# Gates by seven half products and queries channel-major in a hybrid DeltaNet, retention and gated-MLP block

## The chip, the cores and the metric

The kernel runs on one core of a Trainium2 chip. The metric is the device time of one execution in microseconds (us), as the median of several timed runs. One further execution is recorded by the profiler.

The engines are named as in the profile: PE multiplies matrices (PEld is its weight load), DVE and ACT and POOL do the elementwise work, and SP issues most of the DMA transfers. ACT issues the others on a queue of its own.

## The reference

One decoder block over 2048 tokens of width 1024, all in float32:

```python
n = rms_norm(x, attn_norm_w)
gq, gk, gv, gg, ga, gb, rq, rk, rv, rg = split(n @ w_in)      # 512 columns each; ga, gb: 4
o_gdn = gated_deltanet(gq, gk, gv, gg, ga, gb)   # 4 heads of 128
o_ret = retention(rq, rk, rv, rg)                # 4 heads of 128
h = x + concat(o_gdn, o_ret) @ w_out
n2 = rms_norm(h, mlp_norm_w)
g, u = split(causal_conv3(n2 @ w_up))            # 2816 columns each
h = h + (silu(g) * u) @ w_down
return rms_norm(h, final_norm_w)
```

- `gated_deltanet` runs a causal convolution of four taps and silu over q, k and v, normalizes each head's q and k to length 1, and applies the gated delta rule in chunks. Inside a chunk a unit triangular matrix is inverted; from chunk to chunk a 128x128 state per head is carried along. Its output is `rms(o) * norm_w * silu(gg)`.
- `retention` rotates q and k by position (pairs of neighbouring channels, cosine and sine tables) and applies a linear recurrence with a fixed decay per head. Its output is `rms(o) * silu(rg)`.
- `gg` and `rg` together are the 1024 columns of gates that this case is about.

## The kernel before

**Precision.** PE's fast format keeps fewer bits than float32, so every large operand is split into a high and a low part, and a product takes three passes (`mm3`, L116 to L118, and the same three in `tokmajor`, L399 to L401): high times high, high times low, low times high. A split is a copy by ACT and a subtraction by DVE.

**Blocks and items.** The tokens are worked in four blocks of 512 (`TB`), each of four tiles of 128. `mixers` makes, for each block, a dictionary of named items (functions that emit instructions). The string `ORDER` names them in the sequence in which they are emitted: `1p0` is item `p0` of block 1. `hybrid_block` walks this string. An item that needs weights has them loaded (`load_chunk`, into a pool of five `wc` tiles) when the weight-needing item ahead of it starts. A scheduler then places the instructions on each engine by priorities and modelled times, and sizes some pools, so the order on an engine follows `ORDER` only roughly. Matmuls of one block's projections, of the block before and of its output projection are interleaved with the recurrence.

The items of a block, in the order of the data:

- `pro` loads the transposed input (`xk`), scales it by the norm's weights and splits it into eight `n1` tiles (L387). It also sums squares of the input's rows and gets the inverse norm `r` of each token. `rrow`, the same numbers along a row on all partitions, is made by PE: four small matmuls of `r` with the identity (`rrp`, L373) and a copy by ACT.
- `k0`, `q0`, `kq`, `v0`: the retention's projections, token-major (`tokmajor`: tokens on partitions, up to 512 columns in a PSUM bank). Keys and queries are rotated by `rotate`: two DVE multiplications a head and tile (L769, L771) and an addition on POOL (L774).
- `dec`, `d0` to `d3`: decays; each head's decay matrix `D` comes by a broadcast from DRAM on ACT's queue (`D<-gdr`).
- `a0` to `a3` (`proj_kq`): the gated heads' keys and queries, channel-major (`chmajor`: channels on partitions, 512 tokens in a bank). DVE multiplies the bank by `rrow` (L520, `scaled`); the convolution and silu follow.
- `c0` to `c3` (`gdn_kq`): PE transposes keys and queries (`kqtr`, L555), and ACT sums the squares of each (L558); then the products of keys with keys and queries follow (L585). `f`, `e`: values.
- `b0`, `b1` (`gdn_base`): the triangle's inversion for two heads. POOL does its steps (L637, L639); the data goes through DRAM.
- `l0`, `l1` (`gdn_lvls`): the levels of the inverse above 32x32, with small matmuls on PE.
- `r00` to `r13` (`gdn_rec`): the recurrence, eight steps a block, each for two heads. A step is a chain: PE (`ks`), DVE (`kv`, L717), PE (`wps`, L724), DVE (`pers`, L727), PE (`sps`, L732), DVE (state, L734).
- `h0` to `h3`, `y0` to `y3` (`ret_head`, `ret_out`): retention. `ret_head` transposes keys and queries on PE (`rtr`, L826) and copies both by ACT (L827).
- `p0`, `p1` (`gates`): the gates, token-major, 512 columns each. ACT applies silu (L412).
- `g`, `G` (`gated`): norm times gate on DVE (`mix`, L435), transposed by PE (`mxt`, L437). Sums of token halves for the next item are made here (`co`).
- `W1` to `W7`: the output projection by seven products of half size in place of eight (a Strassen scheme over halves of tokens, of inner columns and of output columns). `load_v` makes the differences of weights when a product is first used: subtractions on POOL (`wvt`, L186), a split by ACT and DVE (L213, L214), and a copy kept in DRAM, from which the later blocks load.
- `N`: second norm, transposed, stored to DRAM for the MLP.

A projection's weight is loaded raw and split the first time (`wraw`, 512 KB loads). Its split form is kept in DRAM and loaded back for the later blocks (`wc<-wd`, 512 KB, high and low part). The gates' inner loop shows how often a tile is used: with 512 columns a `wc` tile holds one `k`, and serves 12 matmuls.

```python
for k in range(KT):
    wh, wl = wrow(w, k, ncol)
    for t in range(NT):
        ah, al_ = n1[k][:, 0, t * P:(t + 1) * P], n1[k][:, 1, t * P:(t + 1) * P]
        ps = pss[t][:, :ncol]
        PE.matmul(ps, ah, wh, start=(k == 0), stop=False)
        PE.matmul(ps, ah, wl, start=False, stop=False)
        PE.matmul(ps, al_, wh, start=False, stop=(k == KT - 1))
```

The mixers' items are followed by `mlp_up` (seven half products as well, about 1160 to 1940 us) and `mlp_down` (to the end). The products `W` of block 3 stand at the border.

Of the kernel before, what the change touches and what calls it, by code (L numbers as in the profile page):

```python
# [15 lines left out]
NW = 5  # L16
# [3 lines left out]
NVR = 4  # L20
NVV = 23
NWUR = 2
NST = 4
NUC = 6
NACC = 9
NWU = 9
NWV = 5
# [4 lines left out]
NPR = 2  # L32
NRAW = 3
NLATE = 3
NXR = 7
FD = 5
BUFS = {"n1": 8, "ykq": 5, "kv": 4, "NT": 6, "AT": 8, "o": 4, "n2s": 11, "xk": 2, "og": 1, "co": 7, "Cw": 7,
        "wx": 1, "wsq": 2, "wvr": 3, "wvt": 8, "ca": 8, "mix": 10, "D": 8, "rk": 6, "rq": 3, "rv": 8,
        "Ar": 1, "Nb": 7, "rot": 1, "rrow": 7}

ORDER = ("0pro 0k0 0v0 0dec 0d0 0a0 0c0 0f0 0e0 0q0 0d1 0a1 0c1 0f1 0a2 0e1 0d2 0c2 0f2 0h0 0y0 0b0 0h1 "
# [42 lines left out]
def hybrid_block(ctx, tc, x, xT, w_kq, w_v, w_g, w_rk, w_r0, w_r, w_o, w_u, w_d, cols, rows, fnr, masks, rot, out):  # L84
# [10 lines left out]
    nc.scalar.dma_start(colt, cols)  # L95
# [6 lines left out]
    gnw = colt[:, 204:205]  # L102
    mhalf = base[:, NCOL:NCOL + 16]
# [9 lines left out]
    def mm3(ps, pairs, first=True, chk=False):  # L113
        n = len(pairs)
        for i, (ah, al, bh, bl) in enumerate(pairs):
# [11 lines left out]
           for q in range(2) for i in range(1, 8)}  # L127

    items = mixers(ctx, tc, base, o, marks, drp, mm3, gamma, mhalf, n1w, n2w, gcw, gv127, epsr, gnw, n2d, hd,
                   x, xT, w_kq, w_v, w_g, w_rk, w_r0, w_r, w_o, rows, masks, rot)  # L130
# [28 lines left out]
def load_v(tc, pool, w, i, k, tags, kept=None, drp=None, held=None):  # L159
# [6 lines left out]
    if kept is not None and (i, k) in kept:  # L166
        v = mk("v", F32R)
        nc.sync.dma_start(v.bitcast(F32), kept[i, k])
        return v
# [35 lines left out]
    v = split_v(nc, mk("v", F32R), src)  # L205
    if kept is not None:
        kept[i, k] = drp.tile([P, 2, TB], F32, name=f"wo{i}_{k}", tag=f"wo{i}_{k}", bufs=1)
        nc.sync.dma_start(kept[i, k], v.bitcast(F32))
    return v
# [9 lines left out]
def mixers(ctx, tc, base, base_used, marks, drp, mm3, gamma, mhalf, n1w, n2w, gcw, gv127, epsr, gnw, n2d, hd,  # L219
           x, xT, w_kq, w_v, w_g, w_rk, w_r0, w_r, w_o, rows, masks, rot):  # L220
# [26 lines left out]
    mk = pc(4, P)  # L247
    nc.scalar.dma_start(mk, masks)
    ident = mk[:, 0, :]
    U = mk[:, 1, :]  # L250
    eye8 = mk[:, 2:].rearrange("p a b -> p (a b)").rearrange("p (c i) -> p c i", c=8)


    below = pc(P)
# [1080 lines left out]
```

## Time and profile before

| | before |
|---|---|
| median of 3 timed runs | 2457.25 us |
| the runs | 2455.92, 2462.43, 2457.25 us |
| span of the profiled execution | 2458.5 us |
| PE busy | 2397.2 us, 98% of the span |
| DVE, ACT, POOL busy | 65%, 41%, 22% |
| bytes moved by DMA | 607.29 MB, 247 GB/s on average |

How to read the profile's lines: `x` in front of a number counts instructions. In a line of a group, `out<-in` are names of tiles; behind them stand partitions x elements, the count, the total busy time and the mean duration of one in ns, then the idle time of the engine just ahead of them and what ended it. In a line of waits, `PE tok L399 <- ACT n L387: 9.6, 1, 9.6` says that the instructions of PE that write `tok` at line 399 waited for ACT's `n` of line 387: 9.6 us in total, over 1 wait, of which the longest took 9.6. In a line of a window, each engine's busy time stands beside its number of instructions; behind the engines come PEclk (the granted clock of PE, 1.00 is full), the share in which the DMA engines were busy, and GB/s. In a line of DMA issues, KB of each and median us from issue to landing stand last.

### The profile page before, as it was taken

What the parts mean: (1) busy time and instruction counts of PE and PEld (TensorE: products, weight loads), DVE (VectorE), ACT (ScalarE), POOL (GpSimd) and SP (SyncE); (2) the same over time, 40 slices, a digit from 0 to 9 for tenths busy, and PEclk for the clock granted to TensorE, in tenths of its full rate; (3) what the DMA queues carried; (4) which work ended last, traced back from release to release, by engine and by line L of the source; (5) the groups of instructions that cost most, each with busy time, mean ns of one, the idle gap of its engine ahead of it and who ended that gap; (6) DMA issues with size and microseconds to landing.
All of it is one profiled execution on the core that took longest, in us unless ns stands there. A gap on an engine that the chain in (4) does not pass through costs nothing.

```text
span 2458.5 us, 35801 instructions
## 1 busy us (share of the span) xinstructions
PE 2397.2 (98%) x12476; PEld 2016.0 (82%) x12476; DVE 1596.7 (65%) x3157; ACT 998.8 (41%) x2152; POOL 532.7 (22%) x877
## 2 busy tenths in 40 slices
PE   8998899999999999998999999999999999999998
PEld 7887788788888878887888888888888888888887
DVE  5855777444754563447888988896556577454674
ACT  6644535344442552336454344442122234332341
POOL 1354245621047105240000000000000002421030
PEclk9999999999999999999999999999999999999999
DMA  8856589674765656654998878877667778775773
GB/s 327 277 187 218 214 310 343 223 247 175 268 228 180 211 186 222 224 184 181 349 365 313 303 290 300 290 280 250 233 239 258 270 259 281 243 224 156 220 242 112
DMA packets 287477, 607.29 MB, mean 247 GB/s; under 512 B 41088, under 2 KB 121152, under 8 KB 287296
## 3 DMA queue, kind: packets, MB, share of 16 engines
q1 hardware_dynamic: 270720, 590.70, 68.7%
q10 hardware_dynamic: 16576, 14.30, 1.9%
q8 instruction: 98, 1.61, 0.3%
q14 instruction: 83, 0.68, 0.1%
HBM read 405.32 MB, written 199.59 MB: 246 GB/s over the span
## 4 chain that ended last, share of the span: by engine, by line
PE 84%; POOL 5%; DMA 4%; DVE 3%; issue 2%; ACT 2%; SPq 0%; ACTq 0%; POOLq 0%; DVEq 0%
PE p L116 11%; PE p L118 11%; PE p L117 11%; PE d L118 6%; PE d L116 6%; PE d L117 6%; PE tok L399 4%; PE tok L401 4%; PE tok L400 4%; PE chm L116 3%; PE chm L117 3%; PE chm L118 3%; POOL pers L639 2%; POOL pers L637 2%; PE wo L116 2%; PE wo L117 2%
## 5 line engine op out<-in xcount | busy, mean ns | idle before, releaser
L117 PE MATMUL p<-x,wu 128*128 128x512 f32 x1176 | 457.7, 389 | 0.0
L116 PE MATMUL p<-x,wu 128*128 128x512 f32 x1176 | 452.7, 389 | 0.0
L118 PE MATMUL p<-x,wu 128*128 128x512 f32 x1176 | 450.0, 389 | 0.0
L399 PE MATMUL tok<-wc,n 128*128 128x512 f32 (+2 forms) x768 | 276.5, 365 | 19.5 <-ACT n L387 9.6
L400 PE MATMUL tok<-wc,n 128*128 128x512 f32 (+2 forms) x768 | 276.6, 361 | 1.1 <-DVE wc L296 1.1
L401 PE MATMUL tok<-wc,n 128*128 128x512 f32 (+2 forms) x768 | 275.1, 361 | 0.0
L116 PEld LDWEIGHTS p<-x,wu 128*128 128x128 f32 x1176 | 220.8, 188 | 46.4 <-DVE uc L1053 0.4
L118 PEld LDWEIGHTS p<-x,wu 128*128 128x128 f32 x1176 | 220.8, 188 | 45.8
L117 PEld LDWEIGHTS p<-x,wu 128*128 128x128 f32 x1176 | 220.8, 188 | 45.8
L1095 DVE SCALAR_TENSOR_TENSOR acc<-uc,base,acc 128x1023 f32<-128x1023 f32 (+1 forms) x176 | 221.0, 1280 | 39.2 <-ACT acc L1092 38.9
L1053 DVE TENSOR_TENSOR uc<-p,uc 128x512 f32<-128x512 f32 x224 | 153.6, 689 | 134.8 <-PE p L118 131.6
L186 POOL TENSOR_TENSOR vt<-vr 128x512 f32<-128x512 f32 x44 | 66.0, 1504 | 633.0 <-DMA vr<-in_w_d 465.8
L399 PEld LDWEIGHTS tok<-wc,n 128*128 128x128 f32 x768 | 146.1, 191 | 41.0 <-ACT n L387 9.6
L117 PE MATMUL d<-v,uu 128*128 128x512 f32 x448 | 174.3, 389 | 0.0
L118 PE MATMUL d<-v,uu 128*128 128x512 f32 x448 | 174.3, 389 | 0.0
L116 PE MATMUL d<-v,uu 128*128 128x512 f32 x448 | 174.3, 389 | 0.0
L400 PEld LDWEIGHTS tok<-wc,n 128*128 128x128 f32 x768 | 146.5, 191 | 20.8 <-DVE wc L296 1.5
L401 PEld LDWEIGHTS tok<-wc,n 128*128 128x128 f32 x768 | 145.3, 191 | 19.8
L116 PE MATMUL chm<-n,wc 128*128 128x512 f32 x384 | 151.7, 395 | 0.0
L118 PE MATMUL chm<-n,wc 128*128 128x512 f32 x384 | 151.2, 394 | 0.0
L117 PE MATMUL chm<-n,wc 128*128 128x512 f32 x384 | 150.8, 393 | 0.0
L1092 ACT ACTIVATE acc<-uc,base 128x1024 f32<-128x1024 f32 x88 | 97.2, 1144 | 86.2 <-DVE uc L1053 45.1
(250 smaller groups left out, 4723.3 us busy)
## 6 DMA issues: line engine op xcount, KB each, us to landing
wu<-wu SPq DMA_DIRECT2D x308, 512.0 KB, 5.9
wc<-wd SPq DMA_DIRECT2D x168, 512.0 KB, 5.2
wv<-wo SPq DMA_DIRECT2D x84, 512.0 KB, 5.2
wd<-wc SPq DMA_DIRECT2D x60, 512.0 KB, 4.8
ur<-au SPq DMA_DIRECT2D x56, 512.0 KB, 5.5
wur<-in_w_u SPq DMA_DIRECT2D x44, 512.0 KB, 6.5
au<-st SPq DMA_DIRECT2D x88, 256.0 KB, 4.7
vr<-in_w_d SPq DMA_DIRECT2D x77, 256.0 KB, 5.0
```

What stands on the lines that cost most here:

```text
L116: PE.matmul(ps, ah, bh, start=(first and i == 0), stop=False, skip_group_check=chk)
L117: PE.matmul(ps, ah, bl, start=False, stop=False, skip_group_check=chk)
L118: PE.matmul(ps, al, bh, start=False, stop=(i == n - 1), skip_group_check=chk)
L186: POOL.tensor_tensor(tt[:, j], a, b_, op=ALU.subtract)
L399: PE.matmul(ps, ah, wh, start=(k == 0), stop=False)
L400: PE.matmul(ps, ah, wl, start=False, stop=False)
L401: PE.matmul(ps, al_, wh, start=False, stop=(k == KT - 1))
L637: POOL.tensor_tensor(tm[:, :, :n], Nb[:, j:j + 1, j + 1:].to_broadcast([P, 8, n]), X[:, :, j:j + 1].to_broadcast([P, 8, n]), op=ALU.mult)
L639: POOL.tensor_tensor(X[:, :, j + 1:], X[:, :, j + 1:], tm[:, :, :n], op=ALU.add)
L1053: add = lambda o, ps, a: DVE.tensor_tensor(o, ps, a, op=ALU.add)
L1092: ACT.activation(acc, u, AF.Copy, scale=mcw[:, ci, 2:3])
L1095: DVE.scalar_tensor_tensor(acc[:, t:], u[:, :T2 - t], w, acc[:, t:], op0=ALU.mult, op1=ALU.add)
```

## The change

**Gates.** In blocks 1 to 3 the items `P1`, `P4`, `P6`, `P7`, `P5` replace `p0` and `p1`. They compute all 1024 gate columns by the seven-product scheme (`seven`, `half_product`): a product covers 256 tokens, half of the inner columns and 512 gate columns, 24 matmuls. Its partial sums are put together by DVE from PSUM (`gate_ready` then applies silu). Three of the products read `n1` tiles; four read sums of token and channel halves, which items `S` and `T` (`combos`) make from a second load of the block's `xk`: ACT scales it, DVE adds, ACT and DVE split (tiles `sm`, `sc`). A 512 KB weight tile `wc<-kP` serves six matmuls. Block 0 keeps `p0` and `p1`, with weights read from the new layout.

**Weight differences.** `make` is a new stage: items `O0` to `O3` make all seven forms of the output weights, and `Q0` to `Q3` those of the gates, in block 0's and block 1's time: raw loads, four subtractions on POOL, seven splits by ACT and DVE and seven 512 KB stores to DRAM a stage (56 stores; `load_v` made 28, and 16 splits of the gates' weights were stored). `W1` to `W7` load from there in every block; `load_v` no longer keeps its results.

**Retention queries.** Items `q0`, `q1` compute them channel-major (`ret_q`): no transposes in `ret_head`. The rotation is three DVE operations and an addition on DVE for each head, with transposed tables `rotT`, scaled once a block by `rrow`. For that, each head's channels are permuted, even ones first. `k1` (256 columns) replaces `kq`. Values lie in tiles by token tile.

**Gated queries' norms.** `gdn_kq` no longer transposes the queries. ACT squares them channel-major, DVE transposes 32x32 squares and sums, and a small matmul in `gdn_lvls` (`fold`, `qss`) adds the four bands.

**Smaller edits.** `rrow` comes by a write of `r` to DRAM and a broadcast back on ACT's queue. The masks are loaded behind the fourth `n1` tile (`constants`). The first weights and the first input are loaded in halves, alternating (`first_x`). Pools are resized, and `ORDER` is new.

The diff, cut:

```diff
-NVR = 4
-NVV = 23
+NVR = 2
+NVV = 25
...
-        "wx": 1, "wsq": 2, "wvr": 3, "wvt": 8, "ca": 8, "mix": 10, "D": 8, "rk": 6, "rq": 3, "rv": 8,
-        "Ar": 1, "Nb": 7, "rot": 1, "rrow": 7}
+        "wx": 1, "wsq": 2, "wvr": 2, "wvt": 7, "ca": 9, "mix": 4, "D": 5, "rk": 8, "rq": 2, "rv": 10, "sm": 2,
+        "sc": 11, "wg": 2, "kt": 4, "Ar": 3, "Nb": 6, "rot": 1, "rrow": 4, "rT": 2}
...
+    def make(n, w, kk):
+        def f(_):
+            r = [unit(ap_, "wvr", [P, 2, TB], bufs=BUFS["wvr"]) for j in range(2)]
+            t = [unit(ap_, "wvt", [P, 2, TB], bufs=BUFS["wvt"]) for j in range(2)]
+            for j in range(2):
+                nc.sync.dma_start(r[j].rearrange("p a n -> p (a n)"), w[kk, :, 2 * j * TB:2 * (j + 1) * TB])
...
+            t1 = sub(0, b12, b11)
+            t2 = sub(1, b22, t1)
+            t4 = sub(2, b21, t2)
+            t3 = sub(3, b22, b12)
+            for i, src in ((1, b11), (2, b21), (4, t4), (6, t2), (7, t3), (5, t1), (3, b22)):
+                v = al("wg", [P, 2, TB], F32R)
+                ACT.activation(v[:, 0], src, AF.Copy)
+                DVE.tensor_tensor(v[:, 1], src, v[:, 0].bitcast(F32), op=ALU.subtract)
...
+                nc.sync.dma_start(d, v.bitcast(F32))
...
     def load_chunk(key, src):
+        if key[0] in "PV":
+            for kk in range(4):
+                wc = unit(wp, "wc", [P, 2, TB], F32R, bufs=NW)
+                marks["c"] = nc.sync.dma_start(wc.bitcast(F32), made[key[0]][key[1], kk])
...
-            ps = mbank("rrp")
-            for t in range(NT):
-                PE.matmul(ps[:, t * P:(t + 1) * P], r[:, t:t + 1].to_broadcast([P, P]), ident, start=True, stop=True)
+            rd = drp.tile([NT, P], F32, tag="rd", name="rd")
+            nc.scalar.dma_start(rd.rearrange("t p -> p t"), r)
             rrow = st["rrow"] = half(st, "rr", "rrow", 0)
-            ACT.activation(rrow, ps, AF.Copy)
+            nc.scalar.dma_start(rrow, rd.rearrange("t p -> (t p)").partition_broadcast(P))
...
+        def half_product(i, w, m, ps):
+            prs = []
+            for kk in range(4):
+                if i in (1, 2, 4):
+                    t0 = (2 * (i == 4) + m) * P
+                    n1 = st["n1"][2 * kk + (i != 1)]
+                    ah, al_ = n1[:, 0, t0:t0 + P], n1[:, 1, t0:t0 + P]
+                else:
+                    ah, al_ = (t[:, m * P:(m + 1) * P] for t in st["sc", i][kk])
+                prs.append((ah, al_, w[kk][:, 0], w[kk][:, 1]))
+            mm3(ps, prs, first=i not in (2, 3), chk=i in (2, 3))
...
+                        if i == 1:
+                            ACT.activation(c12[:, m], ps, AF.Copy)
+                        elif i == 2:
+                            ready(0, m, ps)
+                        elif i == 4:
+                            ACT.activation(c21[:, m], ps, AF.Copy)
+                        elif i == 6:
+                            DVE.tensor_tensor(c12[:, m], ps, c12[:, m], op=ALU.add)
+                        elif i == 7:
+                            DVE.tensor_tensor(c22[:, m], ps, c12[:, m], op=ALU.add)
+                            DVE.tensor_tensor(c21[:, m], c21[:, m], c22[:, m], op=ALU.add)
+                            ready(0, 2 + m, c21[:, m])
...
         def gdn_kq(h):
-                for i in range(2):
-                    ps = mbank("kqtr")
+                ps = mbank("kqtr")
...
+                q2 = al("ca", [P, 2, TB])
+                ACT.activation(q2[:, 0], ykq[:, 1], AF.Square)
+                DVE.transpose(q2[:, 1], q2[:, 0])
+                DVE.tensor_reduce(st["qr", h // 2][:, h % 2 * 16:(h % 2 + 1) * 16],
+                                  q2[:, 1].rearrange("p (a d) -> p a d", d=32), axis=mybir.AxisListType.X, op=ALU.add)
...
         def gdn_lvls(hs):
+                ps = mbank("qss")
+                PE.matmul(ps[:, :32], fold, st["qr", hs[0] // 2], start=True, stop=True)
...
-        def ret_kq1(w):
...
+        def ret_q(p):
+            def f(w):
...
+                dst = rot_dst(p, "q")
+                for i in range(2):
+                    ps = chmajor(w, i)
+                    t = al("ca", [P, 2, TB])[:, 0]
+                    DVE.tensor_tensor(dst[i], ps, rT[:, 0], op=ALU.mult)
+                    for o in (0, 64):
+                        DVE.tensor_tensor(t[64 - o:128 - o], ps[o:o + 64], rT[o:o + 64, 1], op=ALU.mult)
+                    DVE.tensor_tensor(dst[i], dst[i], t, op=ALU.add)
...
         def ret_head(h):
-                for i, s in enumerate((k, q)):
-                    ps = mbank("rtr")
-                    for c in range(NT):
-                        PE.transpose(ps[:, c * P:(c + 1) * P], s[:, c * P:(c + 1) * P], ident)
-                    ACT.activation(kq[:, i], ps, AF.Copy)
+                ps = mbank("rtr")
+                for c in range(NT):
+                    PE.transpose(ps[:, c * P:(c + 1) * P], k[:, c * P:(c + 1) * P], ident)
+                ACT.activation(kT, ps, AF.Copy)
```

Block 1 in the two orders, from its first recurrence step to the output products:

```diff
-1r00 1r01 1r02 1b1 1h2 1y2 1r03 1p1 1p0 1l1 1r10 2pro 1h3 1y3 1r11 1g1 1r12 1r13 1g0 2k0 1G1 2dec 1G0 2v0 1W1 1W2
+1r00 1S 1r01 1r02 1h2 1b1 1y2 1r03 1h3 1P1 1l1 1P4 1P6 1T 1P7 1r10 1P5 1g0 1y3 1r11 1r12 2pro 1r13 2v0 1g1 2k0 1G1 2dec 1G0 1W1 1W2
```

More of the change, by code (lines that the diff above doesn't have):

```diff
@@ L204, in load_v @@
             src = sub(0, qs[2], src)
[L205 to L209, printed above, removed]
+    return split_v(nc, mk("v", F32R), src)
 def split_v(nc, v, src):
@@ L245, in mixers, with constants @@
     dtb = rowt[:, 4:8]
-    mk = pc(4, P)
-    nc.scalar.dma_start(mk, masks)
+    mk = pc(5, P)
     ident = mk[:, 0, :]
     U = mk[:, 1, :]
-    eye8 = mk[:, 2:].rearrange("p a b -> p (a b)").rearrange("p (c i) -> p c i", c=8)
+    fold = mk[:, 4]
+    eye8 = mk[:, 2:4].rearrange("p a b -> p (a b)").rearrange("p (c i) -> p c i", c=8)
     below = pc(P)
-    DVE.tensor_scalar(below, U, 1.0, 1e4, op0=ALU.subtract, op1=ALU.mult)
+    def constants(after):
+        with tc.issue_after(after.ins):
+            nc.scalar.dma_start(mk, masks)
+        DVE.tensor_scalar(below, U, 1.0, 1e4, op0=ALU.subtract, op1=ALU.mult)
     ones = pc(P)
@@ L292, in load_chunk @@
                     raw2 = unit(wp, "wraw", [P, 2, step], bufs=NRAW)
-                    marks["w"] = nc.sync.dma_start(raw2.rearrange("p a n -> p (a n)"), src[:, o:o + 2 * step])
+                    for j in range(2) if start and o == 0 else (slice(0, 2),):
+                        a, n_ = (j, 1) if isinstance(j, int) else (0, 2)
+                        marks["c"] = nc.sync.dma_start(raw2[:, a:a + n_].rearrange("p a n -> p (a n)"),
+                                                       src[:, o + a * step:o + (a + n_) * step])
+                        if start:
+                            first_x(o // (2 * step), j)
                 raw = raw2[:, o // step % 2]
@@ L356, in pro1 @@
         def pro1(_):
[L357 removed]
+            ss = small("ssk", 4, 8)
             for t in range(NT):
```

283 lines of the change are left out of this document (195 added, 88 removed), and 21 rows, old and new, of the table ORDER.

## The prediction

> **What bounds the kernel now.** I read first the page's busy lines and its chain of work, then the windows by stage, then what TensorE (PE) waited for.
>
> ```profile
> span 2458.5 us, 35801 instructions
> PE 2397.2 (98%) x12476; PEld 2016.0 (82%) x12476; DVE 1596.7 (65%) x3157; ACT 998.8 (41%) x2152; POOL 532.7 (22%) x877
> GB/s 327 277 187 218 214 310 343 223 247 175 268 228 180 211 186 222 224 184 181 349 365 313 303 290 300 290 280 250 233 239 258 270 259 281 243 224 156 220 242 112
> ```
> ```profile
> core 0: us, PE busy (x) PEld busy (x) DVE busy (x) ACT busy (x) POOL busy (x), PEclk, DMA share, GB/s
> 60.00:120.00 60.00, 60.00 (x333) 52.22 (x332) 49.88 (x121) 37.19 (x101) 15.85 (x21) 1.00 0.82 280
> 220.00:320.00 100.00, 92.02 (x653) 80.52 (x653) 77.15 (x223) 62.64 (x173) 19.70 (x20) 0.99 0.66 239
> 341.00:350.00 9.00, 9.00 (x48) 7.73 (x48) 7.30 (x20) 2.44 (x4) 6.40 (x10) 1.00 0.92 359
> 500.00:600.00 100.00, 98.43 (x703) 87.53 (x702) 43.69 (x148) 47.09 (x141) 17.37 (x40) 1.00 0.61 209
> 1060.00:1145.00 85.00, 80.75 (x679) 69.63 (x677) 44.63 (x126) 41.77 (x120) 17.93 (x44) 1.00 0.41 137
> 1145.00:1290.00 145.00, 137.75 (x614) 113.59 (x613) 129.79 (x206) 76.23 (x129) 10.79 (x15) 0.96 0.93 352
> 1290.00:1910.00 620.00, 619.98 (x2735) 513.15 (x2734) 485.12 (x682) 223.36 (x310) 25.26 (x35) 1.00 0.77 276
> ```
> PE is busy for 98% of the span. The mean duration of a matmul overlaps its neighbours, so the price of one is its pitch: the window from 1290 holds nothing but 128x512 matmuls without a pause, 620 us / 2735 = 0.227 us each. The four mixer blocks fill the first 1145 us, the MLP up to the end; the change lies in the mixers. What PE loses there is small and spread:
>
> ```profile
> PE tok L399 <- ACT n L387: 9.6, 1, 9.6
> PE sps L732 <- DVE pers L727: 6.4, 11, 0.9
> PE mxt L437 <- DVE mix L435: 5.8, 2, 5.0
> PE tok L399 <- ACT mix L412: 5.4, 1, 5.4
> PE wps L724 <- DVE kv L717: 4.8, 8, 1.4
> ```
> The first is the start, two hold single stalls of about 5 us, the rest are hops of the gated recurrence. So the time is PE work plus small waits: removed PE work is time saved, if nothing else comes late.
>
> **PE work that goes.** From the instruction lists of the two built programs, PE has 208 matmuls and transposes fewer (11,364 to 11,156).
>
> ```profile
> 694.35 0.87 PE kqtr L555 x8
> 829.59 0.89 PE rrp L373 x8
> 842.40 0.87 PE rtr L826 x8
> ```
> Gates: 192 matmuls of 512 columns a block become 7 x 24 = 168 in three blocks, 72 x 0.227 = 16.3 us. Transposes of both kinds of queries: 64 each, at 0.87/8 = 0.109 us, 14.0 us. The row of inverse norms (rrp): 32 records, 32 x 0.111 = 3.6 us. Added: eight folds of 16 squares' sums, two records each, not in the trace; between nothing and the 0.111 of rrp a record, 0 to 1.8 us, I take 0.5, since they move 32 columns, not 128. The retention projections keep their columns: 96 matmuls of 256 and 96 of 512 a block stand before and after. PE work: 16.3 + 14.0 + 3.6 - 0.5 = **33.4 us less**.
>
> **The start.** PE waits 9.6 us for the first scaled tile, whose load is this step of the chain:
>
> ```profile
> 1.65 7.06 DMA xk<-in_xT
> ```
> It now follows half a weight tile, is half as long, and the masks (which competed with it) wait. Full size it took 7.06 us; a 256 KB load's median is 4.8 (`wx` below). So -2.3 us from the load, and half a microsecond from its earlier place in the queue; but block 0's later loads stay behind 327 GB/s in the first slice and may hand it back. I take -3, bounds -5 and +1.
>
> **Weight loads of the gates.** A 512 KB weight tile served 12 gate matmuls (2.7 us of PE), now six (1.36 us).
>
> ```profile
> wc<-wd SPq DMA_DIRECT2D x168, 512.0 KB, 5.2
> wx<-in_x SPq DMA_DIRECT2D x32, 256.0 KB, 4.8
> wraw<-in_w_r SPq DMA_DIRECT2D x14, 512.0 KB, 7.5
> ```
> From the first to the last gate matmul of blocks 1 to 3 I add up the pitches of what stands between them in PE's list, since the recurrence and other products are interleaved: 65, 83 and 64 us (0.227 a 512-column matmul; 9 us / (48 records at 341) gives only an upper 0.19 for the 256-column ones, half of 0.227 a lower; the rest 0.109 to 0.22). In the same stretches the lists load 24.1, 25.7 and 22.8 MB. The best slices moved 349 and 365 GB/s, the first 327. At 365 that needs 66, 70 and 62 us, at 327 74, 79 and 70: PE waits 1 us or, at the slow end, 9 + 0 + 6 = 15. Each tile's buffer is free a median of 9.7 us of PE work ahead of its use (five buffers), more than the 5.2 us of a kept tile and the 7.5 us of the crowded first loads; only six or so tiles have under 5. I take +5.
>
> For that rate the Trainium skill ("DMA: Bandwidth & Descriptors", Specifications) gives some 358 GB/s a core from HBM; by it the three stages would need 67, 72 and 64 us, +2 in place of +5. The trace goes above it, 365 GB/s over a whole slice, reads and writes together.
>
> **Other engines.** From the lists, DVE gets 198 more instructions of 512 elements, 84 of 256 and 16 transposes, less 60 us: the rotations of queries (128 instructions) and the old splits of differences.
>
> ```profile
> L520 DVE TENSOR_TENSOR ca<-chm,rrow 128x512 f32<-128x512 f32 x48 | 33.0, 688 | 28.6 <-PE chm L118 26.6 <-ACT ykq L533 1.3 <-PE tok L401 0.4
> L442 DVE TENSOR_TENSOR co<-og,co 128x256 f32<-128x256 f32 x16 | 6.7, 419 | 3.5 <-ACT co L440 3.3 <-ACT og L440 0.2
> L650 DVE STREAM_TRANSPOSE NT<-AT 128x512 f32<-128x512 f32 x16 | 11.3, 710 | 26.9 <-DMA AT<-z 26.9
> L769 DVE TENSOR_TENSOR pers<-tok,rot 128x128 f32<-128x128 f32 x128 | 36.7, 287 | 51.2 <-PE tok L401 23.2 <-POOL rk L774 15.2 <-POOL rq L774 11.8
> L774 POOL TENSOR_TENSOR rq<-rq,pers x64: 452/462/911, 77.1 to 1053.2; 128x128 f32<-128x128 f32 x64
> D<-gdr ACTq DMA_DIRECT2D x16, 256.0 KB, 5.6
> ```
> 198 x 0.688 + 84 x 0.419 + 16 x 0.71 - 60 = +123 us, some 64 of them before 500 us. In the windows above DVE is busy 83%, 77%, 44% and 53% of the mixers; 123 more over 1145 us is 11 points, so DVE stays below PE, but a hop of the recurrence can stand behind one 0.69 us instruction. Against that, PE no longer waits for ACT to copy queries, and POOL loses 64 adds of 0.462 us, 30 us, of which the differences of the gates' weights take most back. I take +4 for these waits, bounds -5 and the rival's below. The stage of differences costs PE nothing while its queues run ahead: 56 writes of 512 KB stand on SP's queue where 28 and 16 stood, and SP's next loads stand behind them; if that cover goes, each is one 5.2 us landing. The row of norms goes through DRAM: a write and a broadcast as long as `D<-gdr`, 5.6 us. Behind it wait the scalings of the first gated products (L520); k0's 96 narrow matmuls, over 11 us, cover it. Gated levels now wait on PE for the folded sums, with the triangle's small matmuls queued behind; the two DVE instructions before were done long earlier (0 us, at most the 0.7 of one).
>
> **Sum.** 2458.5 - 33.4 - 3 + 5 + 4 = 2431.1 us on the profiled execution. Only its span is recorded; the timed runs' median is 1.25 lower, so **2430 us**. A measurement of this kernel tells about 0.3% (7.4 us) from no change: same means 2449.9 to 2464.6.
>
> **Rivals.**
>
> *A. Late gate weights and a slowed clock: about the same time.*
>
> ```profile
> 213.00:218.00 5.00, 0.00 (x0) 0.00 (x0) 0.86 (x3) 0.57 (x2) 3.59 (x15) 0.81 0.00 0
> 218.00:223.00 5.00, 4.68 (x11) 3.72 (x12) 2.28 (x4) 3.99 (x10) 0.40 (x1) 0.51 0.20 46
> 1145.00:1150.00 5.00, 0.14 (x2) 0.00 (x0) 2.83 (x10) 2.73 (x10) 1.65 (x2) 0.79 1.01 399
> 1150.00:1158.00 8.00, 6.72 (x20) 5.47 (x21) 8.00 (x20) 5.85 (x13) 0.00 (x0) 0.50 0.62 238
> ```
> After each stall of 5 us PE's granted clock was about 0.5 for 5 and 8 us, which costs 2.5 to 4 us more. If the loads run at 327 GB/s, the 15 us of waiting may come as four stalls of nearly 4 us and cost 4 x 3.5 = 14 more: 2430 + 10 + 14 = 2454. For it speaks the halved PE time per tile; against it the 9.7 us of lead and that waits of 2 us left the clock alone. The Trainium skill ("TensorE: Matmul & The Clock Gate", Part 1) has the clock halve after an idle window of some 3.4 us; both stalls here agree. Chance 0.12.
>
> *B. The recurrence waits behind DVE's new work: slower.* Each of 32 recurrence steps passes DVE three times, and PE has to wait when the fillers are used up. Today 8 + 11 of these hops wait (the two rows above, 11.2 us). If each of 96 hops stood behind one more 0.688 us instruction, that is 66 us: 2430 - 4 + 66 = 2492. It decides against the change (over 2464.6) from 0.40 us a hop. For it: DVE's 83% and 77% before 320 us, and fewer transposes on PE to fill in. Against: DVE at 44% and 53% in the later recurrences, where gate products now stand between the hops. Chance 0.12.
>
> *C. The stalls go as well: faster still.* With POOL relieved of query adds while it inverts triangles (3.59 of 5 us in the row at 213), that stall and its half clock (5.4 + 2.5) may go, the load waits with it (5), and the 4 us of new hops need not come: 2430 - 17 = 2413. Chance 0.10.
>
> **Numbers.** Forecast 0.66, its own range 2418 to 2449. Low end 2412 (C), high end 2458 (A and its surplus); outside lie B and the rest of C, under 0.2. Faster 0.66 + 0.10 + 0.02 of A = 0.78; same 0.10 of A = 0.10; slower 0.12.
>
> **What would show it.** In the profile after: 208 fewer PE matmuls and transposes; the first PE wait near 7 us; waits of the gate products (P) on DMA under 15 us; one or two half-clock places, not five; waits of `wps` and `sps` for DVE under 20 us. Wrong: P waits with PEclk near 0.5 in three stages (A), or `wps`/`sps` waits of 40 us and DVE above 90% before 320 us (B).

## The result and the profile after

The changed kernel takes 2497.0 us (median of four timed runs, 2489.8 to 2500.7) against 2457.7 before. The ratio is 1.0157, with a 95% interval of 1.0136 to 1.0177: some 39 us slower, where 27 us faster were forecast. The profiled execution has a span of 2492.7 us against 2458.5.

From the page of the changed kernel, the span, the busy time of each engine, and the granted clock and GB/s in 40 slices:

```profile
span 2492.7 us, 35671 instructions
PE 2392.7 (96%) x12260; PEld 2000.8 (80%) x12260; DVE 1718.8 (69%) x3315; ACT 1051.5 (42%) x2109; POOL 529.3 (21%) x817
PEclk9998899999999999998999999999999999999999
GB/s 321 350 197 251 284 339 307 325 328 211 269 250 231 289 185 213 249 304 213 351 326 330 306 304 292 277 293 238 228 286 254 212 280 232 245 203 176 228 258 101
```

PE has 216 records fewer (12476 to 12260: 72 + 128 + 32 less 16 of the folds), and DVE 122 us more work, as forecast. But PE's busy time fell by 4.5 us only, and in three slices the granted clock is under 0.9.

What PE waited for after the change (columns as before: total, times, longest):

```profile
PE chm L119 <- DVE rk L923: 6.7, 1, 6.7
PE mxt L580 <- DVE mix L578: 6.7, 2, 6.1
PE sps L883 <- DVE pers L878: 6.6, 7, 3.3
PE tok L539 <- ACT n L449: 5.6, 2, 5.4
...
PE chm L119 <- DMA wc<-wd: 4.1, 1, 4.1
PE wps L875 <- DVE kv L868: 3.8, 5, 2.2
PE ttps L824 <- DVE pers L820: 3.7, 1, 3.7
...
PE P L119 <- DMA wc<-kP: 1.3, 2, 1.1
```

The half products waited 1.3 us for their weights, and the recurrence's `sps` hardly more than before. What is new is a number of single waits of 2 to 7 us in many places.

To put the whole in one sum, each matmul in the trace was given its undisturbed pitch (227, 122, 120, 111, 90 and 50 ns for 512, 264, 256, 128, 64 and 32 columns). What a pitch exceeds that is a wait where PE is idle, slow clock where the granted clock is 0.5, and else a short hesitation:

| us | PE work | waits | short | slow clock | first matmul at |
|---|---|---|---|---|---|
| before | 2381.9 | 52.6 | 1.4 | 5.2 | 9.6 |
| after | 2348.6 | 99.9 | 8.7 | 22.0 | 5.4 |
| difference | -33.3 | +47.3 | +7.3 | +16.8 | -4.2 |

The sum is +33.9 us, against +34.2 in the spans. PE's work fell by what was forecast (33.4) and the start gained 4.2 (forecast 3). The two terms for waits that were forecast at +9 together (5 for weight loads, 4 for other engines) came out at +71.

### The profile page after: what moved, and what is told of

Read it like the earlier page. It is cut to its first block, busy times and chain, and to the rows that moved or that the text cites. A ratio compares the mean times of both kernels' runs of the same rounds, so it can differ in the third digit from the quotient of the medians.

```text
span 2492.7 us, 35671 instructions
## 1 busy us (share of the span) xinstructions
PE 2392.7 (96%) x12260; PEld 2000.8 (80%) x12260; DVE 1718.8 (69%) x3315; ACT 1051.5 (42%) x2109; POOL 529.3 (21%) x817
## 4 chain that ended last, share of the span: by engine, by line
PE 68%; DMA 13%; POOL 7%; DVE 6%; ACT 3%; issue 3%; SPq 0%; ACTq 0%; POOLq 0%; DVEq 0%
PE p L121 10%; PE p L119 10%; PE p L120 10%; PE d L121 4%; PE d L119 4%; PE d L120 4%; PE chm L119 3%; PE chm L121 3%; PE chm L120 3%; POOL pers L782 3%; POOL pers L784 2%; DMA vr<-in_w_d 2%; PE wo L119 2%; PE wo L120 2%; PE wo L121 2%
## 5 line engine op out<-in xcount | busy, mean ns | idle before, releaser
L119 PE MATMUL chm<-n,wc 128*128 128x512 f32 x512 | 204.8, 400 | 11.3 <-DVE rk L923 6.7
L121 PE MATMUL chm<-n,wc 128*128 128x512 f32 x512 | 203.0, 397 | 1.2 <-DVE wc L358 1.2
L120 PE MATMUL chm<-n,wc 128*128 128x512 f32 x512 | 202.4, 395 | 0.0
L539 PE MATMUL tok<-wc,n 128*128 128x512 f32 (+2 forms) x448 | 145.8, 342 | 10.9 <-ACT n L449 5.6
L540 PE MATMUL tok<-wc,n 128*128 128x512 f32 (+2 forms) x448 | 149.1, 335 | 0.4 <-DVE wc L358 0.4
L541 PE MATMUL tok<-wc,n 128*128 128x512 f32 (+2 forms) x448 | 145.4, 336 | 0.0
L782 POOL TENSOR_TENSOR pers<-Nb,pers 128x248 f32<-128x248 f32 (+30 forms) x248 | 124.5, 502 | 80.1 <-DMA Nb<-z 62.8
L784 POOL TENSOR_TENSOR pers<-pers 128x248 f32<-128x248 f32 (+30 forms) x248 | 124.9, 504 | 18.1
L1268 POOL COPY base<-uc 128x2 f32<-128x2 f32 x44 | 33.9, 770 | 441.9 <-DVE uc L1221 429.1
```

Source lines behind the costliest of these rows:

```text
L119: PE.matmul(ps, ah, bh, start=(first and i == 0), stop=False, skip_group_check=chk)
L120: PE.matmul(ps, ah, bl, start=False, stop=False, skip_group_check=chk)
L121: PE.matmul(ps, al, bh, start=False, stop=(i == n - 1), skip_group_check=chk)
L782: POOL.tensor_tensor(tm[:, :, :n], Nb[:, j:j + 1, j + 1:].to_broadcast([P, 8, n]), X[:, :, j:j + 1].to_broadcast([P, 8, n]), op=ALU.mult)
L784: POOL.tensor_tensor(X[:, :, j + 1:], X[:, :, j + 1:], tm[:, :, :n], op=ALU.add)
```

## Where the new waits come from

**One stop read closely.** The largest new wait, of 6.7 us, in the changed kernel's timeline. Each line has the start, the duration and the instruction, and in brackets how long the engine was idle before it and what ended that:

```profile
861.37 0.19 ACT L891 ACTIVATION_READ_ACCUMULATOR pers<-o 128x1 f32 x1
871.42 0.34 ACTq L437 DMA_DIRECT2D rrow<-rd  x1
871.81 0.22 ACT L599 ACTIVATE pers<-pers 128x16 f32<-128x16 f32 x1 [10.25 <-DMA rd<-pers]
873.60 0.18 DVE L604 TENSOR_SCALAR pers<-pers 128x32 f32<-128x32 f32 x1 [11.13 <-ACT pers L602]
874.32 0.79 PE L119 MATMUL chm<-n,wc 128*128 128x512 f32 x1 [6.72 <-DVE rk L923]
```

The row of norms is written to DRAM by a DMA (`rd`) and read back by a second one (`rrow`). Both are issued by ACT. The second must not start before the first has landed, so ACT, which takes its instructions in order, stands at it for 10.3 us. DVE has a small instruction at the head of its queue that needs a result of ACT, and stands too. Behind that one wait the rotations that free PE's banks, and PE stops. This row itself was first used at 876.9 us.

The views of the two lines in the changed kernel, first L435, which issues the write, then L437, which issues the broadcast. The first shows who stood for the write; both show how long their DMA took to land:

```profile
ACT pers L599: 10.3, 1
ACT wc L357: 5.5, 1
DMA to landing us min/median/max: 10.1/14.9/18.9
```
```profile
DMA to landing us min/median/max: 3.1/3.8/5.2
```

**The row itself comes late as well.** A block earlier DVE stops. It is to scale the tables of the retention's rotation by the row (`rT`), the row has not landed, and a step of the recurrence stands behind `rT`:

```profile
585.29 1.29 DVE L950 TENSOR_TENSOR rT<-rT,rrow 128x512 f32<-128x512 f32 x2 [11.22 <-DMA rrow<-rd]
586.98 0.71 PE L883 MATMUL sps<-pers,kv 128*128 128x128 f32 x4 [3.33 <-DVE pers L878]
```

**The clock.** Windows of the changed kernel, each of 3.41 us followed by the next, then one pair of the kernel with two parts undone (`rr_mlp`, below), then one of before:

```profile
284.90:288.32 3.42, 1.16 (x8) 0.97 (x8) 2.57 (x9) 1.18 (x2) 0.00 (x0) 1.00 0.89 146
288.32:291.73 3.41, 3.31 (x15) 3.31 (x16) 1.47 (x3) 1.38 (x6) 0.00 (x0) 0.50 0.86 303
868.58:871.99 3.41, 0.00 (x0) 0.00 (x0) 0.00 (x0) 0.18 (x1) 0.00 (x0) 1.00 0.14 41
871.99:878.82 6.83, 4.50 (x11) 3.54 (x12) 5.21 (x22) 3.95 (x9) 2.39 (x3) 0.50 0.17 41
```
```profile
270.09:273.50 3.41, 1.54 (x12) 1.30 (x12) 3.38 (x10) 3.03 (x8) 0.38 (x1) 0.99 0.37 154
273.50:276.91 3.41, 3.41 (x18) 3.41 (x18) 3.13 (x9) 0.66 (x2) 0.00 (x0) 0.51 0.00 0
```
```profile
267.40:270.80 3.40, 1.71 (x15) 1.51 (x15) 2.74 (x16) 3.36 (x7) 1.80 (x4) 1.00 0.00 0
```

A window in which PE is busy for 1.2 us, or 1.5, is followed by one at half clock; one with 1.7 us busy was not. In the traces of all twenty kernels of this study the clock was halved in 169 places, not counting the last of each. Each time PE had been idle for at least 1.42 us of the 3.41 us before. Counted from PE's first matmul, no window with over 1.96 us of idleness went without; between the two both happened. So a wait of 2 us that falls into one window can cost 3.7: itself, and half of the window behind it if PE has work there. The changed kernel has twelve such places, the kernel before two.

## The experiments

All ratios are to the kernel before, timed on the same chip in the same rounds. The theory at the start was R: an engine that has to issue a DMA behind another one's landing stands, and what is queued behind it stands too. Its rivals were V (the work added to DVE delays PE's dependent steps), G (the half products bring waits of their own) and P (the MLP's buffer counts). O, W and F were formed later.

### The row, the pools, the gates and DVE's work

Four kernels, each the changed one with one edit.

`rr_mm`: the row by PE again.

```diff
-            nc.scalar.dma_start(rd.rearrange("t p -> p t"), r)
-            nc.scalar.dma_start(rrow, rd.rearrange("t p -> (t p)").partition_broadcast(P))
+            for t in range(NT):
+                PE.matmul(ps[:, t * P:(t + 1) * P], r[:, t:t + 1].to_broadcast([P, P]), ident, start=True, stop=True)
+            ACT.activation(rrow, ps, AF.Copy)
```

> The changed kernel with one part undone: the row of inverse norms is again made by four small matmuls a block and copied by ACT, not written to DRAM and broadcast back. Theory R (the broadcast is issued from ACT's own queue and makes ACT stand until the write has landed: ACT was idle 5.5 us at 48 us and 10.3 us at 862 us, and PE then 6.7 us): the stall of PE at 874 us and its 6.8 us at half clock go, 3.6 us of PE work come back, 2497 - 6.7 - 3.4 + 3.6 - some 2 in block 0 = 2488. Theory V (the elementwise work added to DVE stands ahead of PE's dependent steps): nothing changes but the 3.6 us, 2497 to 2501. By either theory the stalls at 193 and 197 us stay.

Measured: 2468.6 us, ratio 1.0042 (1.0026 to 1.0059), 28 us less than the changed kernel. The direction is that of theory R, and the size is three times what was expected of it. At the row's two stops shown above PE lost 12 us (waits of 6.7 and 3.3, and 2.3 of the 4.5 us that it worked at half clock); the other 16 are not traced to the row, and the new list of instructions was also placed anew.

`q_plain`: the rotation left out.

```diff
                     DVE.tensor_tensor(dst[i], ps, rT[:, 0], op=ALU.mult)
-                    for o in (0, 64):
-                        DVE.tensor_tensor(t[64 - o:128 - o], ps[o:o + 64], rT[o:o + 64, 1], op=ALU.mult)
-                    DVE.tensor_tensor(dst[i], dst[i], t, op=ALU.add)
```

> The changed kernel without the rotation of the retention's queries: of the four DVE instructions a head and block only the cosine product is left (48 DVE instructions of 0.69 us fewer, 33 us); this part of the computation is left out, and PE's instructions are the same. Theory V (DVE's added work stands ahead of PE's dependent steps; at 193 and 197 us the triangle's levels waited 2.8 and 3.7 us behind these very instructions, with 13.7 us at half clock): 2497 - 6.5 - 6.8 - a few us in the other blocks = 2478 to 2484. Theories R (row by DRAM) and P (pools): 2493 to 2501.

Measured: 2515.0 us, 1.0231 (1.0213 to 1.025). With 33 us less work on DVE the kernel is 18 us slower still, above what either theory asked for; theory V has no room for that. In its timeline ACT again stands for the write, and longer at the costly place:

```profile
884.52 0.34 ACTq L437 DMA_DIRECT2D rrow<-rd  x1
884.91 0.60 ACT L987 ACTIVATE Ar<-rtr 128x512 f32<-128x512 f32 x1 [10.14 <-DMA rd<-pers]
```

PE waited 9.6 us for that `Ar`, and 17.1 us at half clock began there.

`gates_tok`: `p0` and `p1` in all blocks, no `P`, `S`, `T` and `Q` items, split weights kept in DRAM.

> The changed kernel with the gates of all four blocks token-major again (two products of 512 columns a block where the seven half products stood, split weights kept in DRAM; no sums of token halves, no differences of gate weights). PE work rises by 72 matmuls, 16.3 us. If the waits of blocks 1 to 3 come from the half products (their loads, sums and DVE additions): PE's waits and half clock in blocks 1 to 3, which rose by some 33 us against before, fall by half or more, 2497 + 16 - 17 to - 30 = 2483 to 2496. If they come from elsewhere: 2509 to 2515.

Measured: 2511.9 us, 1.0215 (1.02 to 1.0231), 15 us over the changed kernel: the 16 us of PE work came back, and PE's waits did not fall (103.9 us against 99.9).

`mlp_pools`:

```diff
-NVR = 2
-NVV = 25
+NVR = 4
+NVV = 23
...
-NST = 6
+NST = 4
...
-NACC = 8
+NACC = 9
...
-NXR = 8
-FD = 7
+NXR = 7
+FD = 5
```

> The changed kernel with the buffer counts of the MLP as before (raw and split down weights 4 and 23, sums 4, accumulators 9, inputs 7, and the earlier fence for the down projection's first loads). Theory P (the waits at 2150 to 2300 us, 6 us and their half clock, come from fewer raw buffers for the down weights): they go, 2497 - 8 = 2489, and the mixers keep their times. Otherwise 2495 to 2500.

Measured: 2485.2 us, 1.011 (1.0094 to 1.0125), 12 us less. The waits of PE behind 1940 us, first in the changed kernel and then in this one:

```profile
PE d L119 <- ACT u L1341: 2.4, 2, 1.8
PE d L121 <- DVE u L1342: 2.2, 4, 0.7
```
```profile
PE d L121 <- DVE u L1342: 0.9, 1, 0.9
```

In the mixers the stalls are those of the changed kernel (2.9 and 3.7 us at 192 and 196 us, 5.1 at 764, 7.6 at 879). So theory P holds for some 8 us of the 12, the waits and the slow clock of the down projection; the diff had these counts, and the prediction did not cost them.

### Both together, the row alone, and a repeat

> The changed kernel with the row of norms by PE again and the buffer counts of the MLP as before, both undone together. The row alone gave 2468.6, the counts alone 12 less than the changed kernel. If these are separate causes: 2468.6 - 9 = 2457 to 2461. If the gain of the counts was a gain of the mixers' new timing: 2466 to 2470.

Measured: 2463.0 us, 1.0013 (1.0004 to 1.0023), between the two cases. The gains alone were 28 and 12 us; together they are 35 of the 39 us, so they nearly add.

`rr_mlp_qplain` is `rr_mlp` with the edit of `q_plain`.

> As rr_mlp, and the rotation of the retention's queries is left out (only the cosine product stays, 48 DVE instructions of 0.69 us fewer); PE's instructions are those of rr_mlp. With the row's trip out of the way, theory V (DVE's added work stands ahead of PE's dependent steps) expects 10 to 20 us under rr_mlp: about 2440 to 2448. If DVE's added work is not what is left: within 5 us of rr_mlp.

Measured: 2467.4 us, 1.0024 (1.0012 to 1.0036), within 5 us of `rr_mlp`. Theory V gets no support here either.

`before_row` is the kernel before with the two DMAs for the row, the reverse of `rr_mm`'s edit.

> The kernel before with one part of the change alone: the row of inverse norms by a write to DRAM and a broadcast back on ACT's queue, in place of 32 matmul records and four copies. Theory R (ACT stands between write and broadcast, 5 to 15 us a block, and PE behind it): PE's 3.6 us go and 10 to 30 us of waits and half clock come, 2457.5 + 6 to + 26 = 2464 to 2484. If the 28 us of rr_mm were a chance of the new order of instructions: 2454 to 2459.

Measured: 2487.7 us, 1.0111 (1.0096 to 1.0126): 27 us for this part alone, above the range of theory R. What ACT and PE waited for in it:

```profile
ACT ykq L826 <- DMA rd<-pers: 14.5, 1, 14.5
ACT co L439 <- DMA rd<-pers: 10.3, 1, 10.3
```
```profile
PE tok L398 <- ACT co L439: 8.4, 1, 8.4
PE ks L713 <- ACT ykq L826: 8.0, 1, 8.0
```

The two stops of ACT lead to two waits of PE of 8 us. Around each the clock was halved for 10.2 us, of which PE worked 5.6 and 5.8 us. 16.4 us of waits and half of 11.4 make 22 us. In the sums below, the waits and the slow clock of this execution are 34 us above those of before, so 12 lie elsewhere; four more half-clock places (151, 270, 315 and 905 us) are away from the stops. For the 22 us theory R is shown in its own lines.

`control` exchanges two items in the order, `0O0 0y1` for `0y1 0O0`.

> The changed kernel with two neighbouring items of block 0 in the written order exchanged that do not depend on each other (the first stage of output weight differences and the second retention head's output). The same work: how far a mere other order of instructions moves the time. By theory R the stops of ACT stay, 2490 to 2505. If order alone explains 28 us, a spread of that size may show here.

Measured: 2498.2 us, 1.0153 (1.0138 to 1.0168). The scheduler gave PE, DVE, ACT and POOL the same order as in the changed kernel, so this is a repeat of it and says nothing on orders.

### Another queue, and the other parts undone

`row_pool_mlp` is `mlp_pools` with one more edit:

```diff
-            nc.scalar.dma_start(rrow, rd.rearrange("t p -> (t p)").partition_broadcast(P))
+            nc.gpsimd.dma_start(rrow, rd.rearrange("t p -> (t p)").partition_broadcast(P))
```

> The changed kernel with the MLP's buffer counts as before, and with the row's trip through DRAM kept, but its second half (the broadcast, which has to wait for the write) issued by POOL, not by ACT. Without the queue's change this kernel took 2485.2. Theory R (what costs is that ACT stands at the head of its queue until the write has landed): ACT's stops of 5 to 10 us go, POOL stands instead where it has slack, and PE has 3.6 us less than with the row by PE (2463.0): 2456 to 2466. If the cost is that the row itself comes late (DVE's scalings wait for it): 2478 to 2488.

Measured: 2486.2 us, 1.0105 (1.009 to 1.012), the same as with ACT. Theory R asked for 2456 to 2466; the time lies in the range of the other case, that the row itself comes late. The trace shows two things. POOL stands now, and DVE behind it:

```profile
878.90 0.63 POOL L437 DMA_DIRECT2D rrow<-rd  x1 [12.43 <-DMA rd<-pers]
880.05 0.29 DVE L921 TENSOR_TENSOR pers<-tok,rot 128x128 f32<-128x128 f32 x1 [10.63 <-POOL rk L926]
```

PE lost 8.3 us at this place: POOL's key additions free the tiles that DVE's rotation writes. And DVE stands for the row itself, longer than in the changed kernel:

```profile
588.30 1.29 DVE L950 TENSOR_TENSOR rT<-rT,rrow 128x512 f32<-128x512 f32 x2 [13.97 <-DMA rrow<-rd]
589.99 1.22 PE L883 MATMUL sps<-pers,kv 128*128 128x128 f32 x4 [5.63 <-DVE pers L878]
```

So theory R, with ACT as the only place, was too narrow. What costs is the wait for the write, and for the row, at the head of whichever queue has other work behind it.

Three kernels undo one part each on `rr_mlp`: `rr_mlp_gt` the gates, `rr_mlp_kq` the gated queries' norms, `rr_mlp_qt` the retention queries.

> As rr_mlp (row by PE, MLP's counts as before; 2463.0), and the gates of all blocks token-major again. PE work rises by 16.3 us. Theory G (the stages of the half products, where PE's waits and half clock are 27 us above those of before in the three stretches, cause these waits by their loads, sums and additions): 13 to 25 us of it go, 2454 to 2466. If the waits come from the recurrence's other hand-offs and the seven products pay in full: 2474 to 2481.

> As rr_mlp, and the gated queries' sums of squares again by PE transposes and ACT (64 transposes more, 16 small records fewer: 6.5 us of PE work come back; DVE has 32 instructions of 0.7 us fewer and no fold stands in front of the levels). If the fold's wait (3.5 us at 743 us and one slowed window) is a price of this part: 2463 + 6.5 - 5 to - 10 = 2460 to 2465. If not: 2467 to 2472.

> As rr_mlp, and the retention's queries token-major again, with the rotation by DVE and POOL in small pieces and transposes on PE (64 transposes, 7.0 us of PE work come back). If the channel-major queries pay in full: 2468 to 2472. If their large DVE instructions, their scaled tables or their banks cost waits: 2453 to 2464.

Measured: 1.0039 (1.0024 to 1.0054), 1.0037 (1.0024 to 1.005) and 1.0044 (1.0028 to 1.0061). Against `rr_mlp` that is 6.4, 5.9 and 7.6 us more (differences of the ratios times 2458), with intervals of some 4 us. The gated queries' norms pay in full. `rr_mlp_qt` has more PE work than its expectation says: with two token-major items of 256 columns, 768 matmuls of 256 stand where 384 of 512 stood, 5.0 us by the pitches, so 7.6 of some 12 us came back. The gates give back 6 of 16. For theory G the time lies between its two ranges. In the three stretches of the half products (480 to 605, 725 to 920 and 1050 to 1185 us) PE's idle time fell from 35 to 21 us, but two new stalls appeared (8.6 us at 633 us, and 6.1 at 752, inside the second stretch), each with 13.7 us at half clock.

### Is it the order?

Undone one at a time, the parts are worth 20 us together, and `rr_mlp` is no faster than before.

`rest_only` takes all of these edits together (it and `rr_mlp_qt` have one buffer more for transposed queries). `old_order` is `rr_mlp` with the items in the order of before; `old_bufs` is `rr_mlp` with the mixers' old counts. `before_kq` is the kernel before with the edit of `gdn_kq`, `gdn_lvls` and its constants alone.

> The changed kernel with everything undone that saves PE work and the two causes found: row of norms by PE, MLP counts as before, gates token-major, both kinds of queries transposed on PE again. What is left of the change is the new order, the mixers' buffer counts, the stage of output weight differences, the halved first loads and the later masks; PE's work is within some us of before. Undone one by one on rr_mlp, the three parts cost 6.4, 5.9 and 7.6 us where their PE work is 16.3, 6.5 and 7.0. Theory O (order, counts and the difference stage cost waits of their own): the three add up, 2463 + 20 = 2478 to 2486, some 22 us over before with the same work. Theory W (the waits belong to the new parts): near before, 2456 to 2466.

> As rr_mlp (2463.0), with all new parts, but with the items in the order of the kernel before: the half products of the gates stand where its gate projections stood, the narrow key and query items where its joint item stood, and the difference stages at places like those of the change. PE's work is the same. Theory O, as far as it is the order: 10 to 20 us less, 2443 to 2453. If it is not the order: 2458 to 2475.

> As rr_mlp (2463.0), but the mixers' tags that both kernels have get the buffer counts of before (decay matrices 8 for 5, values 4 for 6, and so on). Theory O, as far as it is the counts: 2445 to 2455. If it is not: 2458 to 2470.

> The kernel before with one other part of the change alone: the gated queries' sums of squares by ACT, DVE and a fold in place of 64 PE transposes (6.5 us of PE work less). If a part that only removes PE work pays in full in the old order: 2457.5 - 6.5 = 2449 to 2453. If its wait in front of the levels and two slowed windows eat it: 2455 to 2462.

Measured: `rest_only` 1.0156 (1.0139 to 1.0173), `old_order` 1.0184 (1.0165 to 1.0203), `old_bufs` 1.0112 (1.0097 to 1.0127), `before_kq` 1.0147 (1.0132 to 1.0163). None came out as expected: `rest_only` is 12 to 20 us slower than theory O asked for, neither the old order nor the old counts help the new parts (they cost 42 and 24 us), and a part that removes 6 us of PE work makes the kernel before 36 us slower, though the same part pays in full in the new order. Five of the 12 to 20 us are the narrower query matmuls. Against `rr_mlp`, `rest_only` takes 35 us more and has 34.8 us more PE work, with waits and slow clock almost the same (98.9 and 96.0 us). So the three parts together do pay in full in this order, and theory W falls: the waits are there without the new parts. The sums over PE's pitches:

| us | PE work | waits and short | slow clock |
|---|---|---|---|
| before | 2381.9 | 54.0 | 5.2 |
| rr_mlp | 2352.1 | 77.6 | 18.4 |
| before_row | 2378.3 | 73.3 | 19.5 |
| before_kq | 2375.6 | 80.9 | 16.0 |
| rest_only | 2386.9 | 79.1 | 19.8 |
| old_order | 2352.1 | 112.0 | 23.5 |

`old_order` owes much to one place. PE waits 13.6 us at 270 us, in a stretch of 44.4 us at half clock. The chain of work there, as the profile infers it, runs through a store of weight differences and a load that SP issues when that has landed:

```profile
PE yps L817 <- DVE NT L796: 17.9, 4, 13.6
```
```profile
257.66 8.62 DMA kW<-wg
266.29 0.30 SPq L794
266.64 1.86 DMA AT<-z
269.20 0.71 DVE NT L796
269.96 1.26 PE yps L817 x32
```

That store belongs to the new stage `make`. All kernels that were made from the changed one have it for the output weights, and none leaves it out, so its share in their waits is not tested. The same holds for the halved first loads and the later masks.

In `before_kq` one stall stands out, 11.2 us at 468 us with 13.7 us at half clock. Its lines in the timeline of DVE and POOL, and PE's wait:

```profile
449.92 0.17 DVE L355 COPY pers<-ca 128x3 f32<-128x3 f32 x1
465.64 1.26 POOL L187 TENSOR_TENSOR wvt<-wvr 128x512 f32<-128x512 f32 x1
466.93 0.35 DVE L594 SCALAR_TENSOR_TENSOR NT<-kk,pers,D 128x128 f32<-128x128 f32 x1 [16.85 <-POOL wvt L187]
```
```profile
PE vtr L607 <- DVE AT L597: 11.2, 1, 11.2
```

DVE stands for 16.9 us with an instruction that reads nothing of POOL's. It starts as POOL ends a subtraction of output weights, which stood behind POOL's triangle inversion. That the new tile lies in memory that the weight tile held is likely, since pools are packed by the scheduler, but it is not shown. The edit leaves this instruction as it was; that only its placement changed is argued.

The last two kernels move one item of before and change nothing else: `1h0` ahead of `1f2`, and `2h2` ahead of `3pro`.

> The kernel before with one item moved and nothing else: retention head 0 of block 1 stands a few items earlier in the written order, ahead of the projection of the third gated value. Same instructions, same work; the placement on the engines differs in that region. Theory F (the order before is fitted so closely that any other placement makes some engine stand at the head of its queue behind another one's long work): 8 to 35 us slower, 2466 to 2493. If what cost in the other kernels belongs to their parts and not to a new placement: 2453 to 2463.

> The kernel before with one other item moved: retention head 2 of block 2 ahead of the prologue of block 3. Same instructions, same work. Theory F: 2466 to 2493. Otherwise 2453 to 2463.

Measured: 1.0038 (1.0024 to 1.0052) and 1.0018 (1.0008 to 1.0027), 9 and 4 us slower with the same work. Theory F holds in sign for both; the first reaches its range, the second does not. The first has two new half-clock places (behind 3.4 us of waiting for ACT at 627 us, and at 870 us). Both cost far less than the 36 us of `before_kq`, so that a new placement alone makes such sums is not shown.

No version beat the kernel before.

## Why the prediction was wrong, step by step

- **PE work that goes** was right: 33.3 us by the pitches, 33.4 forecast.
- **The start** was right: first matmul at 5.4 us, 4.2 earlier, forecast 3 with bounds -5 and +1.
- **Weight loads of the gates** lay within the bounds: PE waited 1.3 us for `kP`, forecast 5 with bounds 0 and 15. Undone alone on `rr_mlp`, the half products gave back only 6 of their 16 us, but PE's waits for DMA were small in both kernels (4.0 and 2.6 us).
- **The row of norms** is the step that failed first. The prediction costed it at one landing of 5.6 us and asked who needs the row: the scalings, covered by `k0`. So it had no term in the sum. It did not ask what is queued behind the second DMA on the engine that issues it. It also left out one user of the row, the scaling of `rT`, with the recurrence behind it. The broadcast was sized well (3.1 to 5.2 us), but the write landed after 10.1 to 18.9 us, not 5.6. It is a store of 512 single numbers, and the row that was taken (`D<-gdr`) is a broadcast; that this form makes it late is not tested, since no run stores the row in another. Cost: 28 us (`rr_mm`), 27 us alone (`before_row`), of which 12 and 22 us are traced to the row's own stops. For the in-order queues the Trainium skill ("TensorE: Matmul & The Clock Gate", Architectural detail) says that ACT and DVE are strict first-in first-out; the stops above agree. The Trainium skill ("DMA: Bandwidth & Descriptors", Rules for kernel authors) warns that a transfer without a contiguous last dimension becomes one descriptor per element, and tells to rearrange it.
- **Other engines**: the work added to DVE was sized right (122 us, forecast 123), but the term of +4 for waits was far too small. Summed over the views of waits, PE's waits that DVE ended grew from 25 to 53 us. They did not shrink when 33 us of DVE work were left out (54 us in `q_plain`; 36 in `rr_mlp_qplain` as in `rr_mlp`), so the amount of that work is not what made them, as far as kernels that are placed anew can tell. The MLP's counts were not costed at all (12 us, 8 of them in the down projection).
- **The clock** in rival A was read wrongly. From two long stalls, and from waits of 2 us without effect, it concluded that it takes a stall near 4 us. Idleness of about half of a 3.41 us window was enough (1.42 us at the least, always above 1.96), and short waits in one window add up. Twelve places and 22 us came of that. The Trainium skill ("TensorE: Matmul & The Clock Gate", Part 1) has the clock halve after an idle window of some 3.4 us; that is too mild for this case, where 1.42 to 1.96 us of idleness in a window were enough.
- **The first sentence of the sum**, "removed PE work is time saved, if nothing else comes late", is where the rest went. All nineteen other kernels of this study lie between 3 and 57 us above the kernel before, ten of them with some 30 us less PE work. A part's worth depended on the kernel that it came with: the gated queries' norms gained 6 us in the new order and cost 36 in the old one, and gates, norms and queries gained 35 us together in the new order, as much as their PE work, but only 20 when undone one by one. That a changed list of instructions is placed anew, and that the old placement had fewer stops than all others tried, was not a term of the sum.
- **Rival B** named a number near the measured one (2492) with a mechanism that is not there: the two rows of `wps` and `sps` that made 11.2 us before make 10.4 after (5.0 us of waiting for ACT came to `wps`).

What stays open is why the placement of before is so much better. `rr_mlp` lost 96 us of PE's time to waits, hesitations and slow clock, against 59 before. They are not the work of the three parts, since `rest_only` has them too. That the order and counts of before were fitted to each other fits all runs, but no experiment held the placement fixed while a part changed, and none left out the stage of weight differences, so this is argued, not shown.

## What to carry to other kernels

When a DMA must wait for another one, ask what stands behind it in the queue of the engine that issues it, whoever that is; the store of 512 single numbers took 10 to 19 us in the changed kernel. Ask also which queues the late data itself holds up. When a scheduler places the instructions, a change of the list is also a change of the placement: try a part alone, both in the old order and in the new one, before believing its arithmetic. A wait of 2 us can cost nearly 4.

## What the runs showed of the hardware

Behind PE's first matmul, its granted clock was halved for the next 3.41 us whenever PE had been idle for more than 1.96 us of such a window, and never below 1.42 us (169 places in twenty traces). The same store of 512 single float32 numbers landed after 10.1 to 18.9 us within one execution, and the broadcast that read them back after 3.1 to 5.2 us.
